# A decoder trunk on one core: the residual part of 18 weight tiles made by an adding DMA instead of a vector subtract

## The chip, the core and the metric

The kernel runs on one core of a Trainium2 chip. That core has five engines with a queue of instructions each: TensorE (PE, matrix products), VectorE (DVE), ScalarE (ACT), GpSimd (POOL) and SyncE (SP), and DMA engines that move data between the chip's memory and the core's SBUF. Each engine works through its queue in order; semaphores tie the queues together. PE writes to PSUM, eight banks of 128 x 512 fp32.

The metric is the device time of one execution in microseconds (us), the median over runs. The kernel before takes 1063.82 us (three runs, 1062.98 to 1064.26).

## The reference, cut to what matters

The input `x` is 512 tokens by 1024 channels, fp32. There are two residual layers, each a mixer and then an MLP:

```python
for l in range(2):
    h = rms_norm(x, mix_pre_g[l])
    y = even_mixer(h, ...) if l % 2 == 0 else odd_mixer(h, ...)
    x = x + rms_norm(y, mix_post_g[l])
    h = rms_norm(x, mlp_pre_g[l])
    x = x + rms_norm(sq_relu_mlp(h, mlp_w1[l], mlp_w2[l]), mlp_post_g[l])
```

The change lies in the first mixer:

```python
z = h @ w_in                                # 1024 -> 512 u, 512 q, 512 k, 512 v, 8 forget logits
y_a = s5_mixer(u, ..., w_glu)               # complex state-space scan, gelu, y * sigmoid(y @ w_glu)
y_b = fox_attention(q, k, v, fl, b_f)       # 8 heads of 64, causal, with a cumulative forget bias
return concatenate([y_a, y_b], -1) @ w_out  # 1024 -> 1024
```

The odd mixer has a pooling part and a gated part, the MLPs have 4096 inner channels and a squared ReLU. All results are fp32.

## The kernel before

**Products in three parts.** A product of fp32 matrices is made of three fast ones. Each operand is split into `hi`, its value rounded to the reduced format fp32r, and `lo`, what is left; `mm3` then adds up hi·hi, hi·lo and lo·hi in PSUM. `split` makes the two parts: ACT copies the source into `hi`, DVE subtracts `hi` from the source into `lo`. Activations and weights go through the same `split`.

**Weights.** A weight tile is 128 partitions by 1024 columns, 512 KB. Class `W` takes three buffers of SBUF for it: a raw one, which SP fills by a DMA, and two for the parts. The raw buffer is free again after the split. The list `plan` names all tiles in the order of their use: four tiles of `w_in_even` for v, then those for the steps in `ORDER` (q0, four of u, q1, q2, q3; a q step has one tile for the q and one for the k channels of two heads), two of `w_glu`, eight of `w_out_even` (rows 4 to 7 first), and then those of the MLPs and of the odd mixer. There are 47 buffers of 1024 columns for everything.

**The first mixer.** It starts with the normalization of x in four blocks of 128 tokens (`norm_T`): PE transposes a block, ACT and DVE split it into the parts that all later products read. Then come v (`token_block`), q and k of a pair of heads (`qk_block`), u (`step_u`), the constants of the state-space part on DVE and ACT (`step_z`, `step_c`, `step_o`, `step_e`, `step_t`), the forget bias (`step_f`), four scans over 128 channels each (`s5_run`) and the attention of four pairs of heads, interleaved, and at the end `w_glu` and the output product. POOL has little in it: it sets buffers to zero, and casts the bias rows into the keys (`KF`, two COPY rows per pair of heads).

**What sets the order.** The kernel doesn't issue as it is written. `Program.record` notes each operation (so that nearly every instruction has the line of this helper, L438, in the profile), and `Program.issue` puts them into the engines' queues by a list schedule: at each step of a simulated time it takes, for an engine that is free, the operation of best priority whose inputs are ready and whose buffers are to be had. The priority is made of the place in the program, the length of work behind it (`RANK`) and a bonus by step (`BOOST`, in thousands of ns; `u` for `step_u`, `q0` for the first `qk_block`, `W0` to `W3` for the weights of a phase). `LOOKS` limits how far ahead of its turn an operation may take a buffer, per phase: of SBUF, of PSUM, of SBUF by SP. The queue orders that come out are fixed in the program. The costs that it reckons with stand in `cost`, the times between engines in `LAT`.

## Time and profile before

| what | value |
|---|---|
| median of the runs | 1063.82 us |
| the profiled execution's own time | 1063.45 us |
| its span, first to last instruction | 1061.7 us, mean TensorE clock 0.993 |
| PE busy | 1039.3 us (98%) |
| DVE busy | 792.9 us (75%) |
| ACT busy | 568.5 us (54%) |
| POOL busy | 57.2 us (5%), 112 instructions |
| DMA | 104.53 MB, all transfers of weights issued by SP |

The shares are averages. The first mixer takes somewhat under a quarter of the span, the first MLP goes on to about 590 us, then come the odd mixer and the second MLP. Windows of the span give each engine's busy time in a stretch; a matmul counts as busy from its start to its modelled end, so a short wait between two can hide in PE's busy time. Names in the rows leave out buffer numbers: nearly every buffer is called `b`, a PSUM bank `bank`, the constants `ct`.

### The profile page before, as it was taken

The page shows a single profiled execution, that of the slowest core. Times are in us where ns is not written, and L with a number is a line of the kernel's source. Part 1 is how long each engine was busy: PE and PEld are TensorE (multiplying, and loading weights), DVE is VectorE, ACT ScalarE, POOL GpSimd, SP SyncE. Part 2 cuts the span into 40 slices and gives each one's busy share as a digit, 9 for nine tenths or more (in the row PEclk, how much of TensorE's full clock was granted, in tenths as well). Part 3 has the DMA queues.
Part 4 walks back from the last instruction along what each step waited for, and adds up shares of the span by engine and source line. Part 5 has one row for each costly group of instructions (what it writes and reads, how often), then busy time and mean ns, then how long its engine had stood idle before and what let it go on. Part 6 is the DMA issues. An engine that isn't in the chain of part 4 may idle for free.

```text
span 1061.7 us, 13872 instructions
## 1 busy us (share of the span) xinstructions
PE 1039.3 (98%) x5133; PEld 846.6 (80%) x5133; DVE 792.9 (75%) x1365; ACT 568.5 (54%) x1037; POOL 57.2 (5%) x112
## 2 busy tenths in 40 slices
PE   8999899999999999999999799999999999999996
PEld 5789677788988888888888688889888888888885
DVE  6968899759856586677778998566776697686786
ACT  5474978546744563553653644445645544553641
POOL 4001000003000000000001310011000000000001
PEclk9999999999999999999999899999999999999999
DMA  8221012623314322422514533306134225223212
GB/s 254 68 80 40 2 40 81 218 60 119 120 40 131 120 72 66 143 85 78 160 60 132 156 100 113 106 4 198 39 99 121 98 80 164 75 80 120 79 59 80
DMA packets 110385, 104.53 MB, mean 98 GB/s; under 512 B 9736, under 2 KB 92844, under 8 KB 110318
## 3 DMA queue, kind: packets, MB, share of 16 engines
q1 hardware_dynamic: 110318, 103.66, 31.8%
q8 instruction: 40, 0.66, 0.3%
q14 instruction: 27, 0.22, 0.1%
HBM read 101.55 MB, written 2.10 MB: 98 GB/s over the span
## 4 chain that ended last, share of the span: by engine, by line
PE 89%; ACT 5%; DVE 2%; SPq 1%; issue 1%; POOL 1%; DMA 0%; DVEq 0%; POOLq 0%; ACTq 0%
PE bank L438 89%; ACT b L438 5%; DVE b L438 2%; SPq L438 1%; POOL small L438 1%; DMA b<-in_x_dram 0%; ACT junk L438 0%; DVE small L438 0%; POOL b L438 0%; DVEq L1974 0%; POOLq L1974 0%; ACTq L438 0%; ACTq L1974 0%; DVEq L438 0%; POOLq L438 0%
## 5 line engine op out<-in xcount | busy, mean ns | idle before, releaser
L438 PE MATMUL bank<-b,b 128*128 128x512 f32 (+5 forms) x4684 | 1000.2, 376 | 8.9 <-DVE b L438 8.0
L438 PEld LDWEIGHTS bank<-b,b 128*128 128x128 f32 (+2 forms) x4684 | 810.3, 188 | 182.3 <-DVE b L438 7.2
L438 DVE TENSOR_TENSOR b<-b,b 128x1024 fp32r<-128x1024 f32 (+7 forms) x654 | 483.2, 775 | 128.8 <-ACT b L438 65.2
L438 ACT ACTIVATE b<-b 128x1024 fp32r<-128x1024 f32 (+6 forms) x582 | 376.1, 690 | 261.3 <-DVE b L438 121.9
L438 ACT ACTIVATE b<-bank 128x512 f32<-128x512 f32 (+7 forms) x269 | 131.3, 516 | 148.4 <-PE bank L438 138.2
L438 DVE TENSOR_TENSOR b<-bank,b 128x512 f32<-128x512 f32 (+2 forms) x210 | 120.7, 604 | 50.9 <-PE bank L438 30.9
L438 DVE TENSOR_TENSOR b<-b 128x256 f32<-128x256 f32 (+5 forms) x202 | 91.0, 466 | 36.0 <-PE bank L438 23.9
L438 POOL TENSOR_SCALAR small<-small 128x1 f32<-128x1 f32 x36 | 15.9, 443 | 852.9 <-ACT junk L438 836.7
L438 ACT ACTIVATE junk<-b 128x512 bf16<-128x512 f32 (+1 forms) x32 | 27.0, 843 | 43.5 <-DVE b L438 37.0
L438 PE MATMUL bank<-ct,b 128*128 128x128 f32 (+3 forms) x387 | 43.0, 260 | 5.0 <-DVE b L438 4.5
L438 DVE SCALAR_TENSOR_TENSOR b<-b,small,b 128x1024 f32<-128x1024 f32 (+1 forms) x32 | 36.4, 1150 | 14.8 <-POOL small L438 14.8
L438 PEld LDWEIGHTS bank<-ct,b 128*128 128x128 f32 (+3 forms) x387 | 33.9, 140 | 15.9 <-DVE b L438 6.1
L438 DVE SCALAR_TENSOR_TENSOR b<-b,b 128x512 f32<-128x512 f32 (+2 forms) x28 | 19.0, 686 | 13.9 <-ACT b L438 13.5
L438 POOL TENSOR_TENSOR small<-small,mhalf 128x1 f32<-128x1 f32 x36 | 26.7, 741 | 2.9
L438 ACT ACTIVATE b<-bank,small 128x128 f32<-128x128 f32 (+4 forms) x36 | 19.2, 545 | 7.4 <-DVE small L438 4.5
L438 ACT ACTIVATE junk<-bank 128x512 bf16<-128x512 f32 x16 | 9.5, 594 | 23.3 <-PE bank L438 23.0
L438 DVE TENSOR_REDUCE small<-bank 128x1 f32<-128x128 f32 (+3 forms) x32 | 14.0, 484 | 2.2 <-PE bank L438 2.0
L438 DVE SCALAR_TENSOR_TENSOR b<-b,bank 128x512 f32<-128x512 f32 x16 | 10.9, 681 | 4.8 <-ACT b L438 4.7
L438 POOL MEMSET b<- 128x4 f32 (+4 forms) x27 | 9.2, 375 | 78.7 <-ACT b L438 26.5
L438 DVE TENSOR_SCALAR b<-b,small 128x128 f32<-128x128 f32 (+3 forms) x28 | 9.9, 376 | 1.3 <-POOL small L438 1.1
L438 DVE TENSOR_TENSOR_SCAN b<-b,b 128x512 f32<-128x512 f32 x8 | 9.8, 1221 | 0.2
L438 POOL CAST b<-b 32x512 fp32r<-32x512 f32 (+1 forms) x8 | 5.3, 663 | 65.3 <-ACT b L438 64.9
(41 smaller groups left out, 97.8 us busy)
## 6 DMA issues: line engine op xcount, KB each, us to landing
b<-in_mlp_w_dram SPq DMA_DIRECT2D x128, 512.0 KB, 4.4
b<-in_w_in_even_dram SPq DMA_DIRECT2D x16, 512.0 KB, 6.7
b<-in_w_in_odd_dram SPq DMA_DIRECT2D x12, 512.0 KB, 4.2
b<-in_w_out_even_dram SPq DMA_DIRECT2D x8, 512.0 KB, 3.5
b<-in_w_out_odd_dram SPq DMA_DIRECT2D x8, 512.0 KB, 3.5
b<-in_x_dram SPq DMA_DIRECT2D x7, 512.0 KB, 5.3
out_dram<-b SPq DMA_DIRECT2D x8, 256.0 KB, 2.0
b<-in_s_w_glu_dram SPq DMA_DIRECT2D x2, 512.0 KB, 3.7
```

What stands on the lines that cost most here:

```text
L438: o.ins = o.fn(*args, **kw)
```

## The change

Class `Added` replaces `W` for 18 tiles: the four of u, the eight of q0 to q3, the two of `w_glu` and four of `w_out_even`. The raw tile is loaded by SP and ACT copies it to `hi` as before. Then ACT copies it a second time with a scale of -1 into `lo`, which gives minus `hi`, and a DMA that POOL issues reads the same tile from the chip's memory once more and adds it onto `lo`, which gives the raw value minus `hi`. The subtract on DVE is gone. Each of these tiles has one ACT copy and one DMA more and one DVE instruction less.

The list schedule gets a cost for that DMA, which is issued on POOL. A term of the priority with weight zero (`DUE`) is taken out with the code that worked it out. `LOOKS` and `BOOST` have new values, which sets a new order in all phases.

```diff
-LOOKS = {0: (202, 21, 10), 1: (186, 29, 7), 2: (48, 11, 15), 3: (36, 8, 6)}
+LOOKS = {0: (97, 21, 21), 1: (63, 42, 7), 2: (18, 17, 11), 3: (31, 10, 2)}
...
-    "q1": -20, "q3": -5, "q0": 120, "u": -5, "S5D": -20, "s0": 40, "t": 5, "z": -25, "q2": -25, "a0": 85, "a1": 10,
...
+    "q1": -60, "q3": -15, "q0": 110, "u": 40, "S5D": 15, "s0": 20, "t": 5, "z": -65, "q2": -65, "a0": 55, "a1": 10,
...
         if eng == "POOL":
+            if name == "dma_start":
+                return 1550
...
-                o.prio = (1 - DUE) * (o.prio * (1 - RANK) * UNIT - RANK * o.rank) + DUE * o.due - 1e3 * o.boost
+                o.prio = o.prio * (1 - RANK) * UNIT - RANK * o.rank - 1e3 * o.boost
...
+                    elif o.name == "dma_start":
+                        clock[e] = now + o.ns
+                        dma = max(dma, clock[e]) + 5000
+                        o.end = dma + 3000
...
     class W:
+        by_dma = False
+
...
             SP.dma_start(raw.f().rearrange("p (a b) -> p a b", a=shape[0]), src)
-            split(raw.f(), self.b[0].r(), self.b[1].r())
+            hi, lo = (b.r() for b in self.b)
+            if self.by_dma:
+                act(hi, raw.f(), AF.Copy)
+                act(lo, raw.f(), AF.Copy, scale=-1.0)
+                G.dma_start(lo.rearrange("p (a b) -> p a b", a=shape[0]), src, accum_op=ALU.add)
+            else:
+                split(raw.f(), hi, lo)
...
+    class Added(W):
+
+        by_dma = True
...
-            plan += [rows(we, 256 * k, 2, 0, 512) for k in range(4)]
+            plan += [rows(we, 256 * k, 2, 0, 512) + (Added,) for k in range(4)]
...
-            plan += [rows(we, 0, 8, 512 + 128 * hp, 128), rows(we, 0, 8, 1024 + 128 * hp, 128)]
-    plan += [rows(w_glu[0], 256 * k, 2, 0, 512) for k in range(2)]
-    plan += [rows(w_out_even[0], 128 * k, 1, 0, 1024) for k in (4, 5, 6, 7, 0, 1, 2, 3)]
+            plan += [rows(we, 0, 8, 512 + 128 * hp, 128) + (Added,), rows(we, 0, 8, 1024 + 128 * hp, 128) + (Added,)]
+    plan += [rows(w_glu[0], 256 * k, 2, 0, 512) + (Added,) for k in range(2)]
+    plan += [rows(w_out_even[0], 128 * k, 1, 0, 1024) + ((Added,) if k in (4, 5, 6, 7) else ()) for k in (4, 5, 6, 7, 0, 1, 2, 3)]
```

Three places of the new order follow. In a row stand the helper's line, the operation, the buffer that is written, behind the arrow those that are read, and the shape; the number behind the underscore tells values in one buffer apart.

**ACT at the start, before.** Rows of 128x2x128 are splits of x (blocks i=2 and i=3), those of 128x1024 the `hi` copies of q0's two tiles and of u's tiles, those of 128x512 results of v.

```order
L438 ACTIVATE b33_359<-b35_225 128x1024
L438 ACTIVATE b29_192<-bank5_346 128x2x128
L438 ACTIVATE b31_198<-bank5_346 128x2x128
L438 ACTIVATE b25_183<-bank3_368 128x2x128
L438 ACTIVATE b27_186<-bank3_368 128x2x128
L438 ACTIVATE b36_384<-b38_253 128x1024
L438 ACTIVATE b48_308<-bank0_234 128x512
L438 ACTIVATE b39_400<-b41_262 128x1024
L438 ACTIVATE b29_192<-bank6_402 128x2x128
L438 ACTIVATE b31_198<-bank6_402 128x2x128
```

**The same place now**, two copies to a tile (those of q0, and of the first three tiles of u):

```order
L434 ACTIVATE b34_361<-b35_118 128x1024
L434 ACTIVATE b33_379<-b35_118 128x1024
L434 ACTIVATE b37_400<-b38_120 128x1024
L434 ACTIVATE b36_419<-b38_120 128x1024
...
L434 ACTIVATE b46_495<-b47_227 128x1024
L434 ACTIVATE b45_499<-b47_227 128x1024
L434 ACTIVATE b29_184<-bank2_350 128x2x128
L434 ACTIVATE b31_189<-bank2_350 128x2x128
L434 ACTIVATE b25_168<-bank1_393 128x2x128
L434 ACTIVATE b27_174<-bank1_393 128x2x128
L434 ACTIVATE b29_184<-bank3_427 128x2x128
```

All ten copies, which read five tiles (b35, b38, b41, b44, b47), now stand ahead of the last six splits of x; before, the second and the third tile's copies stood among these splits, and those of the fourth and fifth behind them.

**POOL between the first and the second pair of heads, now.** The COPY rows are `KF` (32 and 64 partitions, into the keys), the DMA rows the adds onto the `lo` parts of q1's two tiles, q2's two and q3's first.

```order
L434 DMA b81_771<-in_w_in_even_dram 128x8x128
L434 MEMSET b148_1007 128x4
L434 MEMSET b140_1037 128x1024
L434 MEMSET b141_1052 128x1024
L434 COPY b136_1165<-b55_764 32x512
L434 DMA b99_1149<-in_w_in_even_dram 128x8x128
L434 COPY b136_1165<-b55_764 64x512
L434 DMA b102_1203<-in_w_in_even_dram 128x8x128
L434 DMA b105_1223<-in_w_in_even_dram 128x8x128
L434 MEMSET b175_1243 128x4
L434 DMA b108_1237<-in_w_in_even_dram 128x8x128
L434 MEMSET b142_1275 128x4
```

Before, this queue held no DMA; the COPY and MEMSET rows stood next to each other.

**DVE at the boundary of the layers, before.** The rows of 128x2x128 are splits of the first token block for the odd mixer, the row of 128x512 is the last `collect` of the MLP, which adds a PSUM bank to a result and so frees the bank.

```order
L438 TENSOR_TENSOR b706_5359<-b707_5303,b705_5345 128x1024
L438 TENSOR_TENSOR b694_5301<-bank5_5348,b693_5281 128x2x128
L438 TENSOR_TENSOR b696_5308<-bank5_5348,b695_5287 128x2x128
L438 TENSOR_TENSOR b384_3299<-bank4_5002,b384_3299 128x512
L438 TENSOR_TENSOR b698_5311<-bank2_5353,b697_5290 128x2x128
L438 TENSOR_TENSOR b700_5321<-bank2_5353,b699_5294 128x2x128
L438 SCALAR_TENSOR_TENSOR b715_5381<-b275_2268,small_123,b692_5164 128x1024
```

**The same place now:**

```order
L434 TENSOR_TENSOR b706_5370<-b707_5321,b705_5355 128x1024
L434 TENSOR_TENSOR b694_5319<-bank3_5358,b693_5299 128x2x128
L434 TENSOR_TENSOR b696_5326<-bank3_5358,b695_5305 128x2x128
L434 TENSOR_TENSOR b698_5329<-bank6_5363,b697_5308 128x2x128
L434 TENSOR_TENSOR b700_5335<-bank6_5363,b699_5312 128x2x128
L434 TENSOR_TENSOR b384_3317<-bank2_5020,b384_3317 128x512
L434 SCALAR_TENSOR_TENSOR b715_5390<-b275_2179,small_124,b692_5182 128x1024
```

The `collect` (into b384) has moved behind the last two splits.

More of the change, by code (lines that the diff above doesn't have):

```diff
@@ L41 @@
 RANK = 0.55
-DUE = 0.0
 ORDER = "f z c q0 a0 u e o q1 t s0 a1 s1 q2 a2 s2 q3 a3 s3".split()
@@ L301, in issue @@
             o.rank = o.ns + max((s_.rank + self.LAT[o.eng][s_.eng] for s_ in o.succs), default=0.0)
-        at = 0.0
-        for o in ops:
-            o.due = at
-            if o.eng == "PE":
-                at += o.ns
-        for o in reversed(ops):
-            own = o.due if o.eng == "PE" or not o.succs else math.inf
-            o.due = min([own] + [s_.due - self.LAT[o.eng][s_.eng] - o.ns for s_ in o.succs])
         for o in ops:
             if o.eng != "SP":
-                o.prio = (1 - DUE) * (o.prio * (1 - RANK) * UNIT - RANK * o.rank) + DUE * o.due - 1e3 * o.boost
+                o.prio = o.prio * (1 - RANK) * UNIT - RANK * o.rank - 1e3 * o.boost
                 if o.banks and o.eng != "PE":
```

8 rows, old and new, of the table BOOST are left out of this document.

## The prediction

> **What bounds the kernel now.** I read the page first, for the busy shares and the chain of waits.
>
> ```profile
> PE 1039.3 (98%) x5133; PEld 846.6 (80%) x5133; DVE 792.9 (75%) x1365; ACT 568.5 (54%) x1037; POOL 57.2 (5%) x112
> PE 89%; ACT 5%; DVE 2%; SPq 1%; issue 1%; POOL 1%; DMA 0%; DVEq 0%; POOLq 0%; ACTq 0%
> ```
>
> TensorE (PE) is busy for 1039.3 of 1061.7 us, and the change leaves its work alone. Time can be won or lost only where PE stands still, or runs below its rate, for want of another engine. Windows of the span show where that is.
>
> ```profile
> core 0: us, PE busy (x) PEld busy (x) DVE busy (x) ACT busy (x) POOL busy (x), PEclk, DMA share, GB/s
> 0.00:50.00 50.00, 46.89 (x202) 32.34 (x203) 40.48 (x158) 26.75 (x55) 10.89 (x25) 1.00 0.59 171
> 100.00:150.00 50.00, 46.20 (x296) 34.54 (x296) 43.96 (x92) 41.50 (x102) 3.44 (x12) 0.97 0.04 12
> 250.00:300.00 50.00, 50.00 (x319) 45.17 (x318) 43.60 (x71) 34.12 (x66) 3.55 (x6) 1.00 0.28 91
> 550.00:600.00 50.00, 44.39 (x196) 35.89 (x195) 44.02 (x65) 26.45 (x46) 6.72 (x15) 0.93 0.47 144
> 130.00:202.00 72.00, 70.42 (x457) 53.01 (x457) 67.61 (x139) 55.81 (x118) 0.42 (x4) 0.98 0.22 72
> ```
>
> PE has gaps at the start, from 100 to 150 us, and at the boundary between the layers (550 to 600); the row at 250 stands for the MLP stretches, where PE is busy for all 50.00. The last row decides: from 130 to 202 us the S5 scans and the attention blocks run together, and DVE is busy for 67.61 of 72.00 us, 94%. That PE shows 70.42 hides its loss, since a matmul that starts a fraction late is counted as a longer one. DVE sets this stretch, with ACT at 55.81 behind it. The chain of waits, here a few of its pieces, shows that just ahead of it ACT is the one.
>
> ```profile
> 115.18 0.31 ACT b L438
> 120.27 0.31 ACT b L438
> 143.41 17.75 PE bank L438 x126
> ```
>
> From 107 to 143 us small ACT copies of 0.31 to 0.8 us end last one after another (those of `step_t`, `step_o` and the first scan); after that the chain lies mostly on PE.
>
> **What moves.** Each of the 18 tiles loses one DVE subtract and gains one ACT copy, both 128x1024. First such pairs over the run, then those inside 130 to 202 us.
>
> ```profile
> L438 DVE TENSOR_TENSOR b<-b,b 128x1024 fp32r<-128x1024 f32 x198 | 239.9, 1222 | 80.2 <-PE bank L438 41.1 <-ACT b L438 30.5 <-issue 7.4
> L438 ACT ACTIVATE b<-b 128x1024 fp32r<-128x1024 f32 x198 | 204.8, 1055 | 100.0 <-DVE b L438 59.8 <-PE bank L438 22.9 <-DMA b<-in_mlp_w_dram 12.3
> L438 DVE TENSOR_TENSOR b<-b,b 128x1024 fp32r<-128x1024 f32 x7 | 8.4, 1218 | 0.0
> ```
>
> That is 18 x 1.222 = 22.0 us off DVE and 18 x 1.055 = 19.0 us onto ACT. Where neither ends last, it is worth nothing. Five places count.
>
> **1. The scans, 130 to 202 us.** The seven subtracts of the third row are the last tile of q3, both of w_glu and the first four of w_out_even, all Added now, so DVE goes to 67.61 - 8.4 = 59.2 us. Seven more copies bring ACT to 55.81 + 7 x 1.055 = 63.2 us: ACT is then the busier one. If it fills the stretch as far as DVE does now, 67.61 / 72.00 = 0.939, the stretch takes 63.2 / 0.939 = 67.3 us, 4.7 less. If the copies fit into ACT's holes (they wait for a load alone, not for the scan), all of DVE's 8.4 us comes off. Between 4.7 and 8.4 I take **-6.5**.
>
> **2. The start.** In the order all ten copies of the first five Added tiles stand on ACT ahead of the last splits of x, which PE needs to go on; before, the tiles' copies stand between those splits.
>
> ```profile
> 20.00:30.00 10.00, 9.52 (x49) 7.65 (x48) 8.84 (x44) 7.49 (x19) 1.72 (x4) 1.00 1.06 322
> 30.00:40.00 10.00, 10.00 (x47) 8.21 (x46) 10.00 (x53) 3.93 (x7) 0.00 (x0) 1.00 0.06 6
> 30.16 0.60 PE L438 MATMUL bank<-ct,b 128*128 128x128 f32 x4
> 30.51 5.75 PE L438 MATMUL bank<-b,b 128*128 128x512 f32 x24
> 26.09 1.06 ACT L438 ACTIVATE b<-b 128x1024 fp32r<-128x1024 f32 x1
> 30.79 0.66 ACT L438 ACTIVATE b<-bank 128x256 fp32r<-128x256 f32 x2 [0.16 <-PE bank L438]
> 16.33 5.17 DMA b<-in_x_dram
> ```
>
> The loads run at 322 GB/s until 30 us and at 6 GB/s after it, so the fifth tile is there at about 30.5. Its two copies (2 x 1.055), half of the ACT row of two splits (0.33) and as much again on DVE give 33.3 us for PE's next matmul. By the order 62 matmuls of 512 columns of v lie ahead of this stop; before, 63 lie ahead of the transposes at 30.16, so PE comes to it then: **+3.1**. The rows of x that are now loaded ahead (the chain waits on x for 5.17 us at 16.33) don't help, as PE only comes to this stop earlier. Lower bound: the fifth tile 1.5 us sooner, as SP wastes less, +1.6. Upper: two adds of 512 KB share the queues with the loads, 2 x 0.52 MB / 322 GB/s = 3.2 us more, +6.3.
>
> **3. PE's stop at 59.4** goes, since the subtract in front of the copy that PE waits for leaves DVE:
>
> ```profile
> 57.69 1.23 DVE L438 TENSOR_TENSOR b<-b,b 128x1024 fp32r<-128x1024 f32 x1 [0.28 <-ACT b L438]
> 58.83 0.42 DVE L438 COPY b<-b 128x512 f32<-128x512 f32 x1
> 59.40 1.16 PE L438 MATMUL bank<-b,b 128*128 128x512 f32 x3 [1.18 <-DVE b L438]
> ```
>
> The copy of 58.83 can then come 1.23 us sooner: **-1.2** (0, if step 2 makes PE that late anyway).
>
> **4. Ahead of `step_t`.** Eight copies of four q tiles (8 x 1.055 = 8.4 us) now stand on ACT just before and between the first pieces of the ACT chain.
>
> ```profile
> 107.23 4.42 ACT L438 ACTIVATE b<-bank 64x128 f32<-64x128 f32 x16 [5.79 <-PE bank L438]
> ```
>
> ACT is idle for 5.79 us there, which hides most of them; the rest has 8.4 - 5.79 = 2.6 us to push the chain, less what begins earlier: **+0.5** (0 to 2.6).
>
> **5. The boundary.** DVE's last `collect` of the MLP now stands behind all four splits of a row block and not behind two.
>
> ```profile
> 592.51 2.50 PE L438 MATMUL bank<-b,b 128*128 128x512 f32 x5 [3.36 <-DVE b L438]
> 591.11 2.01 DVE L438 TENSOR_TENSOR b<-bank,b 128x256 fp32r<-128x256 f32 x5
> ```
>
> Two splits of 2.01 / 5 = 0.40 us are what its bank waits longer: **+0.8** (0 to 0.8, as PE gets the splits sooner in exchange).
>
> **The adds themselves** have no row: no transfer in the trace is issued by POOL. The nearest are the plain loads of the same tiles:
>
> ```profile
> b<-in_w_in_even_dram SPq DMA_DIRECT2D x16, 512.0 KB, 6.7
> b<-in_w_out_even_dram SPq DMA_DIRECT2D x8, 512.0 KB, 3.5
> L438 POOL CAST b<-b 32x512 fp32r<-32x512 f32 (+1 forms) x8 | 5.3, 663 | 65.3 <-ACT b L438 64.9
> ```
>
> An add reads a tile from HBM as a load does, and the lo part besides. Lower bound 3.5 us (idle queues), upper 2 x 6.7 = 13.4 (busy ones, twice the traffic). I take 6.7 while loads run, and cost it at nothing: its cover is the PE work between the copy and the first use of lo. That cover is thin at one spot only: q0's first tile, copied at 26.09, has its lo at 26.1 + 1.1 + 6.7 = 33.9 us, and PE asks for it 11 matmuls of 0.24 (5.75 / 24) after the stop of step 2, at 35.9. On POOL an add waits for its copy, and behind it stand `KF` casts (0.663 us each) and memsets. POOL is busy for 57.2 of 1061.7 us, so I cost the issue at nothing too.
>
> The Trainium skill, "DMA: Bandwidth & Descriptors", section on the anatomy of a DMA of the gpsimd path, fits such a transfer by 2.0 us plus the bytes at 436 GB/s; for 512 KB that is 3.2 us, an estimate, near the 3.5 of the idle queue, and no run here shows it for an adding one. With it the sum stays and the slower rival falls.
>
> Sum: -6.5 + 3.1 - 1.2 + 0.5 + 0.8 = -3.3. The profiled execution took 1063.45 us (span 1061.7 and 1.75 around it), so 1060.15; the median of the runs lies 0.37 above it, which gives **1060.5**.
>
> **Rivals.** A change below 0.2%, 2.1 us, can't be told from none here.
>
> *The gain is given back* (1063.5). ACT fills the scans' stretch only as DVE does now (-4.7), and the start's +3.1 passes to the end whole, step 3 swallowed in it: -4.7 + 3.1 + 0.5 + 0.8 = -0.3. For it: ACT is at 63.2 of 72.0 by the sum above, and the pieces of 0.31 us are ACT's. Against: copies of weights have no input but the load.
>
> *Slower: the adds come one after another and too late for u* (1065.7). Six adds, q0's two and u's four, go out from 27.2 us on. If they run in turn and take t each, the sixth ends at 27.2 + 6 t. PE asks for that lo 113 matmuls of 512 columns after q0's first (27.1 us at 0.24) and some 4 us of smaller ones, at about 67. From t = 6.6 us on PE waits; at 7.5 us for 5.2, so 1060.5 + 5.2. For it: the median of 6.7 of a plain load there, and twice its traffic. Against: loads share 16 engines and overlap, so adds may. The same rule would make the four adds of q tiles near 105 us late for their `qk` blocks.
>
> The Trainium skill, "SBUF — State Buffer", section "Who interferes with whom", says that a transfer issued by GpSimd can be starved of descriptor writing while a DVE instruction holds the port pair they share. DVE's 10.00 of 10.00 us at 30 to 40 would be its place; no trace here shows it.
>
> *A larger gain* (1055.5): all of DVE's 8.4 comes off, and the start is absorbed behind PE's later stops: -8.4 - 1.2 + 0.5 + 0.8 = -8.3. For it: PE's losses from 100 to 150 us.
>
> *The change is not what decides*: new looks and boosts reorder all phases. Against: PE is busy for 50.00 of 50.00 in the MLPs, so reordering there can win nothing and can lose only what buffers hold up. Either sign, within 4 us.
>
> **Chances.** The forecast 0.34, gain given back 0.27, slower by late adds 0.22, larger gain 0.13, reordering 0.04. Faster by over 0.2%: most of the forecast (0.30), the larger gain (0.13) and 0.03 of the rest, 0.46. Within: 0.27, of the second and the fringes. Slower: 0.22 and 0.05 of the fringes, 0.27. The forecast's own range is 1057.5 to 1062.5, by the bounds of steps 1 and 2. To leave out no more than 2 in 10 it reaches to 1055 on the side of the larger gain and to 1067.5 on the other, past the late adds at 7.5 us.
>
> **What would show it.** Step 1: from the first scan to the last the windows hold about 65 us of time, with ACT above 60 us busy and DVE near 59. Step 2: PE stands still for about 3 us near 30, with ACT named. Step 3: no stop at `step_f`'s copy. Step 4: the chain's ACT pieces start not over 1 us later relative to PE. Step 5: the boundary's stop at 4.2 in place of 3.36. Late adds would show as PE waits on a transfer from w_in_even. Wrong is the forecast if DVE's share in the scans stays at 94%, or if PE waits at the start for more than 6 us.

## The result and the profile after

The changed kernel took 1071.28 us in the median (1070.22 to 1073.43, 4 runs), the kernel before 1063.66 (1062.98 to 1064.26) beside it: a ratio of 1.0073 with a 95% interval of 1.0060 to 1.0085. It is slower by 7.6 us. The forecast was 1060.5 and the range ended at 1067.5, so both missed. The profiled execution, the fastest of the four, took 1070.22 us, with a span of 1068.4 against 1061.7 before, so 6.7 us are to be found in the trace.

The page's busy times and the shares of the chain of waits:

```profile
PE 1037.1 (97%) x5133; PEld 846.1 (79%) x5133; DVE 776.9 (73%) x1347; ACT 584.8 (55%) x1055; POOL 81.9 (8%) x130
PE 85%; DVE 6%; ACT 4%; POOL 2%; issue 2%; DMA 1%; SPq 0%; DVEq 0%; POOLq 0%; ACTq 0%
```

The work moved as announced: 18 instructions fewer on DVE and 16 us less (22.0 reckoned), 18 more on ACT and 16 us more (19.0 reckoned). The chain, however, gives 6% to DVE where it gave 2%. The windows, in the form shown of before (PE, weight loads, DVE, ACT, POOL; granted clock; DMA share; GB/s):

```profile
0.00:50.00 50.00, 40.22 (x166) 27.76 (x167) 36.10 (x158) 30.82 (x63) 17.73 (x28) 0.93 0.93 223
138.00:209.00 71.00, 67.61 (x456) 51.49 (x457) 64.76 (x135) 63.19 (x128) 8.85 (x15) 1.00 0.54 137
550.00:600.00 50.00, 43.61 (x197) 35.34 (x197) 41.38 (x60) 25.47 (x45) 6.57 (x12) 0.96 0.44 138
```

The first row carries most of the loss: 40.22 us of PE in the first 50, where there were 46.89, 166 matmuls in place of 202, and a clock of 0.93. The second row is the scans and the attention, aligned by PE's work: 456 matmuls in 71 us, where 130 to 202 us held 457 in 72. The boundary's row is little changed.

To place the rest I lined PE up with itself: each matmul counts for the usual pitch of its shape (the median time from its start to the next one's, in the kernel before), and at equal amounts of such work done I compare when PE got there. A number is how much later (us) than in the kernel before; e1 to e16 are the experiments below.

```
work done (before's time)  after   e1    e2    e3    e5    e6   e16    e9   e10    e7    e8
  20  ( 24.9)               2.5   4.3   0.6   6.0   1.6   1.7   1.1   2.4   4.2  -0.5   0.3
  30  ( 35.0)               9.1   4.3   6.5   6.0   7.8   2.0   1.9   9.3  11.5  -0.6   0.3
  50  ( 55.3)               9.1   5.1   7.3   6.7   7.7   5.3   2.8   9.2  11.5  -0.6   0.2
  70  ( 76.2)               7.9   4.7   8.0   6.5   6.6   4.1   1.6   8.0  10.4  -0.6   0.2
  90  ( 96.1)               9.0   5.0   7.9   6.0   7.7   5.3   2.7   9.1  11.5  -0.6   0.2
 120  (125.0)               8.8   5.9  10.9   6.3   7.4   5.0   2.5   8.9  11.2  -0.6   0.2
 150  (161.4)               8.0  16.6  16.0  11.5   8.3   5.8   3.3  10.5  13.0  -0.4   1.2
 190  (201.8)               7.0  16.8  21.9  11.5   7.3   4.8   2.3   9.5  11.9  -0.4   8.9
 540  (554.4)               6.2  17.7  22.6  12.2   6.5   4.1   2.1   8.8  11.2  -0.4  16.7
 600  (620.5)               7.1  17.7  22.8  12.7   7.4   5.0   3.2   9.7  12.1  -0.1  16.7
1020 (1042.2)               6.4  16.5  22.5  10.5   6.8   4.6   4.1   8.9  11.6  -0.1  16.8
```

So the changed kernel loses 9.1 us in its first 35, wins 1.2 between 35 and 76 us (where the stop at 59.4 was), gives 0.9 back by 125, wins 1.8 in the scans (work 120 to 190), loses 0.9 at the boundary, and wins 0.8 and 0.7 in the two MLP stretches. Where the two kernels give PE its matmuls in another order, the table is no finer than about 1 us: from 76 to 96 us the lag grows from 7.9 to 9.0, and PE has no stop there in either trace. Only the loss at the start is well above that.

The loss at the start, PE's instructions of the changed kernel from 10 to 46 us:

```profile
16.03 1.32 PE L434 MATMUL bank<-ct,b 128*128 128x128 f32 x8 [1.50 <-DVE b L434]
21.61 1.43 PE L434 MATMUL bank<-b,b 128*128 128x512 f32 x5 [0.53 <-DVE b L434]
30.96 2.99 PE L434 MATMUL bank<-b,b 128*128 128x512 f32 x12
38.11 8.14 PE L434 MATMUL bank<-b,b 128*128 128x512 f32 x25 [4.17 <-ACT b L434]
```

PE has worked off what is ready at 33.95 and stands still for 4.17 us, until 38.11, for ACT. ACT in the same stretch:

```profile
26.45 11.35 ACT L434 ACTIVATE b<-b 64x256 f32<-64x256 f32 x14
37.70 2.69 ACT L434 ACTIVATE b<-bank 128x256 fp32r<-128x256 f32 x8
```

The first row is 14 instructions without a gap: four of `step_c` and then the ten 128x1024 copies of five Added tiles. ACT waits for no load there; it is simply not through. Only behind them come the six splits of x that PE needs. And behind the stop TensorE runs at half its rate (windows at 30, 38 and 41 us):

```profile
30.00:40.00 10.00, 5.83 (x25) 4.42 (x24) 9.25 (x51) 10.00 (x17) 6.48 (x5) 0.80 1.13 183
38.00:41.00 3.00, 2.89 (x7) 2.31 (x8) 2.64 (x8) 2.54 (x9) 0.32 (x1) 0.50 1.22 233
41.00:44.00 3.00, 3.00 (x11) 2.39 (x10) 2.90 (x9) 0.00 (x0) 0.00 (x0) 0.71 1.13 206
```

ACT is busy for 10.00 of 10.00 us. A granted clock of 0.50 over 2.9 us and 0.71 over 3.0 costs 2.9 x 0.5 + 3.0 x 0.29 = 2.3 us. That makes 4.2 for the stop, 2.3 for the clock and 2.5 that PE was late already at 25 us: 9.0 of the 9.1. The Trainium skill, "TensorE: Matmul & The Clock Gate", section "What's actually happening", says that the clock falls to half after an idle window of about 3.4 us; the 0.50 behind a stop of 4.17 us agrees with it. The length of a stop doesn't settle it in these traces, though: behind a stop of 2.67 us the kernel before has 0.54 (129 to 132 us), behind one of 1.67 us e6 has 0.62 (56 to 59 us), and behind one of 3.45 us the changed kernel has 1.00 (139 to 142 us).

### The profile page after: what moved, and what is told of

Read it like the earlier page. It is cut to its first block, busy times and chain, and to the rows that moved or that the text cites. A ratio compares the mean times of both kernels' runs of the same rounds, so it can differ in the third digit from the quotient of the medians.

```text
span 1068.4 us, 13902 instructions
## 1 busy us (share of the span) xinstructions
PE 1037.1 (97%) x5133; PEld 846.1 (79%) x5133; DVE 776.9 (73%) x1347; ACT 584.8 (55%) x1055; POOL 81.9 (8%) x130
## 4 chain that ended last, share of the span: by engine, by line
PE 85%; DVE 6%; ACT 4%; POOL 2%; issue 2%; DMA 1%; SPq 0%; DVEq 0%; POOLq 0%; ACTq 0%
PE bank L434 85%; DVE b L434 6%; ACT b L434 2%; POOL small L434 2%; ACT junk L434 1%; DMA b<-in_mlp_w_dram 0%; DMA b<-in_w_in_even_dram 0%; POOL b L434 0%; SPq L434 0%; DVE small L434 0%; DVEq L1982 0%; POOLq L1982 0%; ACTq L434 0%; DVE mag L434 0%; DVE mst L434 0%
## 5 line engine op out<-in xcount | busy, mean ns | idle before, releaser
L434 PE MATMUL bank<-b,b 128*128 128x512 f32 (+6 forms) x4684 | 998.8, 376 | 15.7 <-DVE b L434 9.5
L434 DVE TENSOR_TENSOR b<-b,b 128x1024 fp32r<-128x1024 f32 (+10 forms) x636 | 463.4, 763 | 129.8 <-ACT b L434 83.3
L434 ACT ACTIVATE b<-b 128x1024 fp32r<-128x1024 f32 (+5 forms) x600 | 393.2, 701 | 231.3 <-DVE b L434 115.5
L434 ACT ACTIVATE b<-bank 128x512 f32<-128x512 f32 (+6 forms) x269 | 131.0, 517 | 179.8 <-PE bank L434 178.3
L434 DVE TENSOR_TENSOR b<-b 128x512 f32<-128x512 f32 (+5 forms) x202 | 90.4, 462 | 38.7 <-ACT b L434 21.9
L434 POOL TENSOR_SCALAR small<-small 128x1 f32<-128x1 f32 x36 | 20.3, 565 | 829.3 <-ACT junk L434 808.4
L434 DVE SCALAR_TENSOR_TENSOR b<-b,small,b 128x1024 f32<-128x1024 f32 (+1 forms) x32 | 36.4, 1149 | 13.8 <-POOL small L434 13.8
L434 POOL TENSOR_TENSOR small<-small,mhalf 128x1 f32<-128x1 f32 x36 | 23.1, 641 | 3.0
L434 POOL DMA_DIRECT2D b<-in_w_in_even_dram x12 | 17.4, 1450 | 38.8 <-ACT b L434 32.4
L434 POOL MEMSET b<- 128x4 f32 (+4 forms) x27 | 10.1, 395 | 59.4 <-PE bank L434 25.8
```

The source lines that it names most:

```text
L434: o.ins = o.fn(*args, **kw)
```

## The experiments

Each is timed against the kernel before on the same chip. Where letters stand in the expectations, S is the theory that the start costs the time, T that the order of the tables does as such, D that late or crowding adds do, and P the rival by which DVE doesn't bound the scans.

### Is DVE what bounds the scans? (e7, e10)

e7 is the kernel before, in its own order, without the seven DVE subtracts of the scans (PE reads the hi part in place of lo).

```diff
+NOLO = (16, 17, 18, 19, 20, 21, 22)
...
-            o.ins = o.fn(*args, **kw)
+            if o.tag and o.tag[0] in NOLO and o.eng == "ACT":
+                o.tag[3].t.ap = o.tag[5].t.get()
+            if not (o.tag and o.tag[0] in NOLO and o.eng == "DVE"):
+                o.ins = o.fn(*args, **kw)
```

> The kernel before in its own order, with seven DVE subtracts of 1.22 us left out between 130 and 202 us (the last tile of q3, w_glu, four of w_out_even); PE reads hi where it read lo, so the lo part of these seven tiles is left out of the result. DVE is relieved with no copy and no add in exchange: the most that step 1 can be worth. The prediction's theory (DVE sets this stretch): -6 to -8.4, 1055.5 to 1058. Theory P (PE's own work fills it: a sum of the matmuls' usual pitches there gives 70 us, the stretch with its first stop 76.8): -1 to -3, 1060.8 to 1063.

It took 1063.59 us (10 runs, 1063.13 to 1064.45): ratio 1.000 [0.999, 1.001]. The window that the first step of the prediction went by, in e7:

```profile
130.00:202.00 72.00, 70.41 (x456) 53.10 (x455) 61.22 (x132) 55.41 (x117) 0.42 (x4) 0.98 0.23 74
```

DVE fell from 67.61 to 61.22 us, and PE did 456 matmuls where it did 457. The relief that step 1 priced at 4.7 to 8.4 us is worth nothing by itself. The times in brackets in the table show why. For 30 units of work (120 to 150) PE takes 36.4 us, from 125.0 to 161.4; for the next 40 it takes 40.4. So nearly all that PE loses in this stretch lies ahead of 161 us. The first row is PE of the kernel before, the second its window behind the stop:

```profile
129.82 4.56 PE L438 MATMUL bank<-b,b 128*128 128x128 f32 x25 [2.67 <-DVE b L438]
129.00:132.00 3.00, 2.18 (x8) 2.02 (x9) 2.99 (x5) 2.96 (x4) 0.10 (x1) 0.54 0.00 0
```

The stop of 2.67 us, 1.3 us for the clock behind it (0.54, then 0.89 from 132 to 135 us) and three stops of 0.19, 0.60 and 0.28 us up to 143.4 make 5.1 of the 6.8 us by which 76.8 exceeds 70. e7 has the same stop, of 2.65 us. Of the seven subtracts one stands at 130.19 and the others at 170.45 or later, where DVE is busy but PE doesn't wait for it.

e10 asks the same of ACT, in the changed kernel: the same seven tiles have neither second copy nor add.

```diff
+            if o.tag and o.tag[0] in NOLO:
+                first, other = (o.tag[1], o.tag[2]) if o.args[0].t is o.tag[1] else (o.tag[2], o.tag[1])
+                if o.eng == "POOL" or first.ap is not None:
+                    continue
+                other.ap = first.get()
...
```

> The changed kernel in its own order, but the seven Added tiles of the scans' stretch (the last of q3, w_glu, four of w_out_even) have neither the second copy nor the add; PE reads hi where it read lo, so these tiles' low parts are left out of the result. ACT is relieved of 7 x 1.055 = 7.4 us there. If ACT has taken DVE's place in the scans (the rival of the prediction): 3 to 5 us less, 1066 to 1068.5. Theory P (PE's own work fills the stretch, and neither engine's copies matter): within 1 us of the changed kernel, 1070 to 1072.

It took 1073.08 us (1071.32 to 1075.41), ratio 1.0085 [1.0068, 1.0102]. From work 120 to 190 PE loses 0.7 us where the changed kernel wins 1.8, so freeing ACT brings nothing there either. By 35 us e10 is 2.4 behind the changed kernel; the first 1.7 of it are a hold on DVE that the last section shows.

The 1.8 us themselves are not the tiles' doing. All seven profiles with this order in the scans (the changed kernel, e4, e5, e6, e9, e10, e16) have the same stop of 3.44 to 3.46 us for DVE there, longer than the 2.67 of before. Behind it the same 24 matmuls take 3.13 us in the changed kernel and 4.45 to 5.57 in the other six. PE and the window behind the stop, first of the changed kernel, then of e9:

```profile
140.05 3.13 PE L434 MATMUL bank<-b,b 128*128 128x128 f32 x24 [3.45 <-DVE b L434]
139.00:142.00 3.00, 1.95 (x15) 1.80 (x16) 2.87 (x5) 2.93 (x7) 0.00 (x0) 1.00 0.00 0
140.17 5.55 PE L436 MATMUL bank<-b,b 128*128 128x128 f32 x24 [3.45 <-DVE b L436]
139.00:142.00 3.00, 1.83 (x7) 1.77 (x8) 2.94 (x5) 2.93 (x6) 0.05 (x1) 0.50 0.00 0
```

The clock stayed at 1.00 in this one execution and fell to 0.50 in e9's. So between work 120 and 150 the changed kernel wins 0.8 us, and the five of the others that are in the table lose 0.8 to 1.8; from 150 to 190 all six win 1.0 or 1.1. The full clock there was luck of the profiled execution; what decides it was not tested.

### The start (e4, e5, e6, e16)

e4 puts the six copies of u's first three tiles, and their adds, behind the last six splits on ACT; DVE is left as it is.

```diff
...
+        last = max(i for i, o in enumerate(order) if o.tag == "X" and o.eng == "ACT")
+        late = [o for o in order[:last] if o.tag in ('W2', 'W3', 'W4')]
+        held = set(id(o) for o in late)
+        order = [o for o in order[:last + 1] if id(o) not in held] + late + order[last + 1:]
...
```

> The changed kernel in its own order, but for one edit: the six copies of the first three tiles of u, with their adds, stand behind the last six splits of x and not ahead of them. All 18 tiles stay Added. Theory S: the splits come 6.3 us sooner, PE's stop of 4.17 goes and with it the stretch at half clock: 1064 to 1067. Theories T and D: 1070 to 1072, since neither the rest of the order nor the traffic changes.

It took 1070.94 us (1070.23 to 1073.22), ratio 1.0072 [1.0057, 1.0087]: no better than the change. ACT, then DVE, then PE of e4:

```profile
33.77 1.73 ACT L441 ACTIVATE b<-bank 128x256 fp32r<-128x256 f32 x6
```
```profile
36.75 2.66 DVE L441 TENSOR_TENSOR b<-b,b 128x256 f32<-128x256 f32 x7
39.34 2.07 DVE L441 TENSOR_TENSOR b<-bank,b 128x256 fp32r<-128x256 f32 x6
```
```profile
39.80 8.52 PE L441 MATMUL bank<-b,b 128*128 128x512 f32 x24 [3.44 <-DVE b L441]
```

ACT's splits are done 4 us sooner, but DVE's halves of the same splits stand in its line behind a long run of small instructions of the S5 setup, and come at 39.34. PE's stop is 3.44 us, and its releaser is now DVE. A split has two halves, and the new order had set both back.

e5 moves only four memsets of `step_o` to the head of POOL. e6 moves, on top of that, the six splits ahead on ACT and on DVE.

```diff
...
+        early = [o for o in order if o.tag == "O"]
+        rest = [o for o in order if o.tag != "O"]
+        at = min(i for i, o in enumerate(rest) if o.eng == "POOL" and o.name == "tensor_scalar")
+        order = rest[:at] + early + rest[at:]
# e6 besides:
+        at = max(i for i, o in enumerate(order) if o.tag == "X" and o.eng == "PE")
+        late = [o for o in order[at + 1:] if o.tag == "X"]
+        order = order[:at + 1] + late + [o for o in order[at + 1:] if o.tag != "X"]
...
```

> The changed kernel in its own order, but for four POOL memsets of 128x1024 (for step_o) that go back to the head of POOL's queue, where they stand in the kernel before. Theory M: in the changed kernel they run from 14.06 to 17.7 us, and a small DVE TENSOR_SCALAR of 0.17 us that meets them takes 1.03 us (2.69 to 3.6 in three of the experiments so far), so PE stops for 1.5 to 4 us at 14 to 18 us, with a stretch at half clock behind the longer ones. Without them: no stop at 16 us, 1 to 3 us come back, 1067.5 to 1070. If the memsets have nothing to do with it: 1071.

> The kernel with the early memsets, and with the last six splits of x moved ahead in both queues: on ACT ahead of the copies for u, on DVE ahead of the small operations of step_z and step_e that stood in front of them (moving ACT's part alone won nothing: DVE's part then came at 39 us, behind those). Theory S: now PE's stop near 34 us goes, and the half clock after it: 5 to 6.5 us less than with the early memsets alone, 1061.5 to 1064. Theory D (traffic and lateness of the adds): no gain, since the lo parts of q0 come no sooner, 1067 or more.

e5 took 1070.41 us (1069.09 to 1070.71), ratio 1.0060 [1.0045, 1.0075]: 0.9 to 1.3 us better in PE's progress at 25 and 35 us, 0.9 in the median, where the two intervals overlap. e6 took 1067.20 (1065.92 to 1068.36), ratio 1.0031 [1.0019, 1.0043]. With the splits ahead, PE's lag at 35 us is 2.0 in place of e5's 7.8: **5.8 us of the loss are the splits' place in the two queues**. PE of e5 and of e6:

```profile
37.24 19.92 PE L441 MATMUL bank<-b,b 128*128 128x512 f32 x78 [4.18 <-ACT b L441]
30.13 21.29 PE L444 MATMUL bank<-b,b 128*128 128x512 f32 x90
```

Of the 5.8 us 3.3 come back at 53 us, so that the time lands where theory D had put it (1067 or more), though not for D's reason: the stop that S named is gone. PE, DVE and ACT of e6:

```profile
53.09 0.42 PE L444 MATMUL bank<-ct,b 16*128 16x16 f32 x4 [1.67 <-DVE b L444]
```
```profile
37.85 8.24 DVE L444 TENSOR_TENSOR b<-b,b 128x256 f32<-128x256 f32 x22
```
```profile
46.05 4.85 ACT L444 ACTIVATE b<-bank 64x512 fp32r<-64x512 f32 x8 [6.33 <-DVE b L444]
```

The 22 instructions on DVE are now later, ACT waits 6.33 us for them, and PE for what follows: a new wait, with a slower clock behind it. e16 tests whether DVE is too full there: e6 without the three subtracts of v's tiles at 17 to 22 us (PE reads the hi part).

```diff
+NOLO = (2, 3, 4)
...
+            if isinstance(o.tag, tuple) and o.tag[0] in NOLO:
+                if o.eng == "DVE":
+                    continue
+                o.tag[2].ap = o.tag[1].get()
```

> The kernel with early memsets and splits first (1067.2), less three DVE subtracts of 1.22 us at 17 to 22 us (v's tiles two to four; PE reads hi where it read lo, so their low parts are left out of the result). If DVE's full queue from 10 to 46 us causes the stop near 53 us: it shrinks or goes, 2 to 3.5 us less, 1063.5 to 1065.5. If the adds of u cause it: unchanged, 1066.5 to 1068.

1067.90 us (1067.39 to 1069.72), ratio 1.0037 [1.0025, 1.0049]: the median isn't better. By its time the first expectation failed. In the trace, though, the stop shrinks to 0.87 us and the lag at 55 us to 2.8, as it said; but another wait turns up, and from work 540 on e16 loses 2.0 us where e6 loses 0.5. PE of e16:

```profile
35.56 15.76 PE L449 MATMUL bank<-b,b 128*128 128x512 f32 x67 [0.59 <-DMA b<-in_w_in_even_dram]
52.19 0.41 PE L449 MATMUL bank<-ct,b 16*128 16x16 f32 x4 [0.87 <-DVE b L449]
```

The first fits the thin cover of q0's first tile that the prediction named: e16's first add goes out at 27.85 us, and its adds take 7.7 in the median, which gives 35.55. It is seen only where PE is no longer held up ahead of it. Why the later phases of e16 lose was not settled.

### The adds (e9, e3)

e9 is the changed kernel with adds of 512 bytes in place of 512 KB.

```diff
+            if o.eng == "POOL" and o.name == "dma_start":
+                args = [args[0][0:1, 0:1, 0:128], args[1][0:1, 0:1, 0:128]]
```

> The changed kernel in its own order, but each of the 18 adds moves 512 bytes instead of 512 KB, so lo is left at minus hi nearly everywhere (the low parts of these weights are left out of the result). The order, the copies and the issues on POOL stay. Theory D (the adds' traffic, 9.4 MB, or lo parts that land late): 2 to 6 us less than the changed kernel, 1065 to 1069. Theory S (the order of ACT's and DVE's queues at the start): within 0.7 of the changed kernel, 1070.5 to 1072.

1073.18 us (1069.72 to 1074.20), ratio 1.0078 [1.0060, 1.0096], with the same stop of 4.16 us for ACT: the stop is not of the adds' making, and without their bytes and their lateness the time is no lower. By work 120 PE's lag is 8.9 us, and 8.8 with the full adds; the difference behind that is the clock at 140 us, shown above. The rows of the transfers on the changed kernel's page (count, KB, median us to landing), and its DMA instructions on POOL:

```profile
b<-in_w_in_even_dram POOLq DMA_DIRECT2D x12, 512.0 KB, 7.6
b<-in_w_out_even_dram POOLq DMA_DIRECT2D x4, 512.0 KB, 7.7
b<-in_w_out_even_dram SPq DMA_DIRECT2D x8, 512.0 KB, 7.1
L434 POOL DMA_DIRECT2D b<-in_w_in_even_dram x12 | 17.4, 1450 | 38.8 <-ACT b L434 32.4
```

An add takes 7.6 us to land, 6.7 had been taken and 3.5 to 13.4 bounded; the estimate of 3.2 us that the prediction gave beside it, by the fit of the Trainium skill, "DMA: Bandwidth & Descriptors", section on the anatomy of a DMA of the gpsimd path, is less than half of what was measured. An add occupies POOL for 1.45 us. A plain load of w_out_even beside them takes 7.1 where it took 3.5 before, and 4.3 in e9.

e3 leaves q0 and u plain, with 12 Added tiles.

```diff
-            plan += [rows(we, 256 * k, 2, 0, 512) + (Added,) for k in range(4)]
+            plan += [rows(we, 256 * k, 2, 0, 512) for k in range(4)]
...
+            kind = (Added,) if hp else ()
...
```

> The changed kernel with q0's two and u's four tiles made by copy and subtract again; the twelve later tiles stay Added. Theory S: the start is that of the tables alone, 6 to 7 us come back (the stop of 4.17 and the half clock behind it), the scans keep their 2 us of gain: 1063 to 1066. Theory T: 1070. Theory D: a third of the adds is gone, those in the busiest stretch: 1066 to 1069.

1073.15 us (1071.93 to 1074.49), ratio 1.0086 [1.0069, 1.0102], against what the start's theory expected. The stop at 34 to 38 us is gone. But 6.0 us are lost by 25 us, to the memsets, and a further 5 between work 120 and 150, where the list schedule came out otherwise too: PE stops there for 3.93 and 2.03 us, in place of 3.45 and 1.12. An edit of the tiles moves the schedule with it, so such an experiment doesn't isolate a tile.

### Order without tiles, tiles without order (e1, e2, e8)

e1 keeps the new tables with all tiles plain; e2 keeps the 18 Added tiles with the tables of before.

```diff
# e1
-        by_dma = True
+        by_dma = False
# e2
-LOOKS = {0: (97, 21, 21), 1: (63, 42, 7), 2: (18, 17, 11), 3: (31, 10, 2)}
+LOOKS = {0: (202, 21, 10), 1: (186, 29, 7), 2: (48, 11, 15), 3: (36, 8, 6)}
# and BOOST as before
...
```

> The new LOOKS and BOOST alone: no tile is Added, all 18 are made by copy and subtract, so the arithmetic is that of before in a new order. Theory S (the start: ten copies of 1.06 us stand on ACT ahead of the last splits of x, and PE stops for them): five copies instead of ten, interleaved with the splits as in the kernel before, so the stop of 4.17 us at 34 us is gone; 1063 to 1066. Theory T (the new order itself costs the time, whatever makes lo): 1069 or more. Theory D (the adds' traffic and lateness cost it): no adds, so 1062 to 1065.

> All 18 tiles Added, LOOKS and BOOST of the kernel before. Theory S: in this order eight copies in a row stand ahead of five of the splits as well, so PE stops there again: 1067 to 1073. Theory T: the old order is good, so 1058 to 1062. Theory D: 1068 to 1073, and the loss lies in waits for lo, not at the splits.

e1: 1079.25 us, ratio 1.0143 [1.0128, 1.0159]. e2: 1084.40, ratio 1.0197 [1.0182, 1.0212]. Either half alone is worse than both by 8 to 13 us. e1 is late by 4.3 at the start and loses 10.7 between work 120 and 150, in stops for DVE and ACT such as these two of its PE:

```profile
140.16 4.62 PE L434 MATMUL bank<-b,b 128*128 128x128 f32 x23 [4.17 <-DVE b L434]
168.59 0.79 PE L434 MATMUL bank<-b,b 128*128 128x512 f32 x1 [3.54 <-ACT b L434]
```

That the new order leans on the relief of DVE, and falls behind without it, fits the first of these stops, but was not taken apart. PE of e2:

```profile
36.89 19.84 PE L434 MATMUL bank<-b,b 128*128 128x512 f32 x74 [3.50 <-ACT b L434]
```

The start's stop is there under the old tables too, and is missing in e1 and e3: it comes with Added tiles at the start, not with the new tables.

e8 asks what the adds are worth where no list schedule rearranges anything: before's order, the seven tiles of the scans Added at the place of their copy or, if later, where lo's buffer comes free.

```diff
...
+            if o.tag and o.tag[0] in ADDED and o.eng == "DVE":
+                pass
+            else:
+                o.ins = o.fn(*args, **kw)
+            for n, src, a, lo, raw, _ in spots.get(at[id(o)], ()):
+                self.engines["ACT"].activation(lo.real(), raw.real(), AF.Copy, scale=-1.0)
+                self.engines["POOL"].dma_start(lo.real().rearrange("p (a b) -> p a b", a=a), src, accum_op=ALU.add)
```

> The kernel before in its own order, with the same seven tiles made by the second copy and the adding DMA, both put right behind the tile's first copy; nothing else moves. The prediction's step 1: -4.7 to -8.4, 1055.5 to 1059. Theory P: between -2 and +1, 1062 to 1065. If the adds harm by themselves (late lo, traffic): 1066 or more.

1080.03 us (1078.44 to 1081.26), ratio 1.0152 [1.0137, 1.0167]. PE's two stops for a transfer, and the last of the adds on POOL:

```profile
186.55 5.08 PE L453 MATMUL bank<-b,b 128*128 128x512 f32 x27 [2.54 <-DMA b<-in_w_out_even_dram]
220.42 2.50 PE L453 MATMUL bank<-b,b 128*128 128x512 f32 x5 [6.12 <-DMA b<-in_w_out_even_dram]
```
```profile
209.40 0.85 POOL L456 DMA_DIRECT2D b<-in_w_out_even_dram  x1 [20.27 <-ACT b L455]
```

Here the adds are late: lo's buffer comes free too near to its use, and a subtract of 1.2 us fits there where an add, of 5.8 to 6.9 us in the medians, doesn't. The last one goes out at 209.40, and PE goes on at 220.42. Not all of the 16.7 us is that: from 130 to 225 us PE waits 8.7 us for these adds, and 4.9 for ACT, where it waited 0.7 before.

### The single stop at 59.4 us (e11, e12)

e11 is the kernel before with the subtract of u's fourth tile exchanged with the copy of `step_f` behind it on DVE. e12 makes that one tile Added, its copies in ACT's idle time ahead.

```diff
# e11
+        cut = next(i for i, o in enumerate(order) if o.tag and o.tag[0] == TILE and o.eng == "DVE")
+        nxt = next(i for i in range(cut + 1, len(order)) if order[i].eng == "DVE")
+        order.insert(nxt, order.pop(cut))
# e12
...
+        order = [o for o in order if o is not hi and o is not cut]
+        order.insert(spot + 1, hi)
...
+                self.engines["ACT"].activation(lo.real(), raw.real(), AF.Copy, scale=-1.0)
+                self.engines["POOL"].dma_start(lo.real().rearrange("p (a b) -> p a b", a=a), src, accum_op=ALU.add)
```

> The kernel before, with one pair of DVE instructions swapped: the subtract of u's fourth tile (1.23 us at 57.69) behind the copy of step_f for which PE stops 1.18 us at 59.40. If that stop is worth what the prediction's step 3 says, and PE does not need the tile's lo at once: 0.5 to 1.2 us less, 1062.5 to 1063.2. If the stop is swallowed later, or PE then waits for lo instead: 1063.4 to 1064.2.

> The kernel before with that one tile Added: its first copy moves ahead in ACT's queue, into ACT's idle 5.45 us before 53.8, the second copy and the add stand right behind it, the subtract leaves DVE. One add where ACT idles and the queue is empty. If step 3 holds and the add lands before PE asks (issue near 51.5, 6 to 7.6 us to land, asked for near 59): 1 to 1.4 us less, 1062.4 to 1062.8, faster than both kernels. If the add is late by a us or two: 1063 to 1065, and PE is seen to wait for it.

e11: 1063.39 us (11 runs), ratio 0.9992 [0.9983, 1.0001]. e12: 1063.47, ratio 0.9990 [0.9981, 0.9998]. In both the stop is gone; PE of e12 runs through it:

```profile
53.62 4.21 PE L453 MATMUL bank<-ct,b 128*64 128x128 f32 x110
57.76 1.19 PE L453 MATMUL bank<-b,b 128*128 128x512 f32 x3
59.04 6.74 PE L453 MATMUL bank<-b,b 128*128 128x384 f32 x29
```

Both gain 1.2 us of progress there. The Added tile gains no more than two instructions exchanged.

### The tables of the later phases (e13, e14, e15)

The kernel before, with the new tables for phases 1 and 3 (e13), with u's fourth tile Added besides (e14), and with those of phases 1, 2 and 3 (e15).

```diff
-LOOKS = {0: (202, 21, 10), 1: (186, 29, 7), 2: (48, 11, 15), 3: (36, 8, 6)}
# e13, e14
+LOOKS = {0: (202, 21, 10), 1: (63, 42, 7), 2: (48, 11, 15), 3: (31, 10, 2)}
# e15
+LOOKS = {0: (202, 21, 10), 1: (63, 42, 7), 2: (18, 17, 11), 3: (31, 10, 2)}
# and BOOST of these phases in all three
...
```

> The kernel before with the changed kernel's LOOKS and BOOST for the two MLP phases alone; the first mixer keeps its order, no tile is Added. If the gains of 0.8 and 0.7 us that PE's progress shows in the MLPs of the changed kernel are the tables' own: 1062 to 1063. The prediction's price for the MLPs (nothing to win where PE is busy for 50.00 of 50.00): 1063.4 to 1064.3.

> The same tables with u's fourth tile Added as in the run with that tile alone (0.999 of before). If the two add up: 1061 to 1062.3, below both kernels by more than the noise. If not: 1063 to 1064.

> As the first of these, with the changed kernel's tables for the odd mixer as well, so the boundary between the layers has the changed order (the collect behind four splits). The prediction's step 5: 0.8 us more than without, so 1062.8 to 1064. If the boundary's +0.9 belongs to the late arrival from the first mixer and not to the order: as without, 1062 to 1063.

e13: 1064.59 us, ratio 1.0005 [0.9996, 1.0014]. e14: 1062.66 (11 runs, 1061.66 to 1063.90), ratio 0.9985 [0.9977, 0.9994]. e15: 1065.70, ratio 1.0010 [1.0001, 1.0019]. The new tables of the later phases gain nothing; that of phase 2 costs about 1.1 us (e15 less e13). e15 did not get the order at the boundary that its expectation counts on: in its trace the `collect` still stands between the two pairs of splits (shown under step 5 below). e14 is the fastest of all, ahead of both kernels, but by 0.15%, inside the 0.2% that the prediction counted as no change; with 11 runs its interval does exclude 1. Why it is faster, while e13's tables alone are not, the traces don't show.

## Why the prediction was wrong, by its steps

**Step 2, the start, is the term that decided: +9.1 where +3.1 was written, bounds 1.6 to 6.3.** The prediction saw the right place, the right releaser and the right rows, and reckoned the stop from the wrong end: from the last load's arrival and the two copies behind it. ACT was never waiting for a load. It had four instructions of `step_c` and ten copies to do in line, 11.35 us, and was through at 37.8, not at 33. The stop is 4.17 us, near the expected 3. The half clock behind it (2.3) and a lag of 2.5 at 25 us had not been in the sum at all. e6 shows 5.8 of the 9.1 to be the splits' place; e5 shows about 1 to be the memsets; the rest of the early lag, some 1.6 us, is the new order's and was not taken apart.

**Step 1, the scans, failed in its reason: -6.5 foreseen, -1.8 in the profiled execution, and less elsewhere: with the same order e5 gets -0.1 there, e9 +0.6.** "DVE sets this stretch" was read from a busy share of 94%. e7 takes the seven subtracts away and gains 0.0 us; e10 takes ACT's seven copies away and gains nothing. What PE loses there is one stop of 2.67 us at 127 us, the clock behind it, and three short stops by 143 us; behind 161 us it runs at its pitch, and there most of the relief fell. The prediction had the piece in hand: its chain of waits went through small ACT copies up to 143 us and then lay mostly on PE. Its remark that a late matmul is counted as a long one hid this reading. Its test, "wrong if DVE's share stays at 94%", was met in part (64.76 of 71.00, 91%; near 59 had been expected, and ACT came to 63.19 as reckoned). Even the -1.8 was luck: the changed order has a longer stop at that place, 3.45 us, and only the clock, which did not fall behind it in the profiled execution, made up for it. What ends that first stop sooner was not tried, and 1.7 of the 6.8 us by which the scans exceed PE's pitch stay open.

**Step 3 was right** in mechanism and size: the stop is gone. The lag of the changed kernel, which falls by 1.2 by 76 us and is back at 9.0 by 96, can't show the size, as its PE takes the work in another order; e11 and e12, which keep the order, show the 1.2 at the spot. Over the whole run about 0.1% is left of it.

**Step 4 was harmless as foreseen.** Between 90 and 120 units of work PE's lag goes from 9.0 to 8.8 us, so the eight copies cost nothing that can be told from the +0.5.

**Step 5 was right** in mechanism and size, +0.9 for +0.8. The boundary's two stops in the changed kernel's PE, and the `collect` (the DVE row of 128x512) in the kernel before, in the changed kernel and in e15:

```profile
594.19 1.09 PE L434 MATMUL bank<-ct,b 128*128 128x128 f32 x8 [2.37 <-DVE b L434]
599.30 1.65 PE L434 MATMUL bank<-b,b 128*128 128x512 f32 x3 [4.02 <-DVE b L434]
```
```profile
591.78 0.68 DVE L438 TENSOR_TENSOR b<-bank,b 128x512 f32<-128x512 f32 x1
598.56 0.68 DVE L434 TENSOR_TENSOR b<-bank,b 128x512 f32<-128x512 f32 x1
592.28 0.68 DVE L432 TENSOR_TENSOR b<-bank,b 128x512 f32<-128x512 f32 x1
```

4.02 stands where 3.36 stood, 4.2 had been named. In all three PE goes on 0.05 or 0.06 us after the `collect` ends (592.51, 599.30 and 593.02 us). It starts 1.32 us after the first split in the changed kernel and 0.67 in the kernel before: 0.65 us later, and the stop grew by 0.66. In e15 it starts 0.66 after it, as before, so e15's 1.1 us have another cause, which stays open.

**The adds** cost the changed kernel nothing that e9 could win back, as the prediction had put it. The slower rival had the right sign and the wrong mechanism: adds too late are real in e8, where a stop of 6.12 us names one, but not in the changed kernel. The rival nearest to the truth was the last, "the change is not what decides", with a chance of 0.04 and "within 4 us": e1 and e2 show the order, and tiles that don't fit it, moving the time by 15 and 20 us.

The forecast's own range, 1057.5 to 1062.5, doesn't come out of the bounds that it names: with both bounds of steps 1 and 2 it is 1057.1 to 1065.5. The result lies outside either.

## What to carry to other kernels

A busy share, even 94%, doesn't say that an engine sets the time. Look first where in the stretch PE stands still; an experiment that leaves the engine's work out then settles it, and costs one run. To say when an in-order engine delivers, add up everything in its line ahead of the instruction that is waited for, on each engine that makes a part of it, and then the clock behind the stop; the last input's arrival is only a lower bound. An add took 7.6 us to land, so it needs that much cover, and an idle engine for its copies; where both held (e12), it gained 1.2 us at the spot, and exchanging two instructions did as much. One profiled execution can be lucky: a stop that the clock happens to pass over looks like a gain.

## What had not been expected of the hardware

A small DVE instruction can be held for several memsets of POOL. Around 14 us POOL clears four buffers; DVE has 128x16 instructions beside it, which take 0.17 us elsewhere. DVE of the changed kernel, of e1, of e3 and of e5 (where the memsets come earlier), and POOL of the changed kernel and of the kernel before:

```profile
13.92 1.12 DVE L434 TENSOR_SCALAR b<-b 128x16 f32<-128x16 f32 x2
15.07 0.88 DVE L434 TENSOR_SCALAR b<-b 128x16 int32<-128x16 int32 x1
```
```profile
13.92 2.90 DVE L434 TENSOR_SCALAR b<-b 128x16 f32<-128x16 f32 x2
```
```profile
13.94 3.79 DVE L434 TENSOR_SCALAR b<-b 128x16 f32<-128x16 f32 x2
```
```profile
13.92 0.25 DVE L441 TENSOR_SCALAR b<-b 128x16 f32<-128x16 f32 x2
```
```profile
14.06 3.68 POOL L434 MEMSET b<- 128x1024 f32 x4
```
```profile
L438 POOL MEMSET b<- 128x1024 f32 x5 | 4.6, 958 | 0.0
```

A memset takes 3.68 / 4 = 0.92 us. The two TENSOR_SCALARs take 0.25 us undisturbed (e5) and 0.87, 2.65 and 3.54 us more in the others, which is one, three and four memsets. PE's stop behind them is 1.50, 3.28 and 4.10 us (0.56 in e5). In the kernel before, five memsets of this size, 0.96 us each, and some smaller ones were over by 6.7 us, ahead of these instructions. The early memsets of e5 hold another one: a CAST of 128x128 at 2.82 us takes 3.80, where it takes 0.23 in the changed kernel; by 13 us DVE is level again. One order of instructions can show different holds: the changed kernel and e9 had 1.12 in their profiled runs, e4 and e10, with the same order there, 2.90. This fits the wide spread of the kernels of that order (1069.7 to 1075.4 us, e5 1069.1 to 1070.7), to which the clock in the scans may add its part. The Trainium skill, "SBUF — State Buffer", section "Who interferes with whom", says that DVE's two-port modes, which a tensor_scalar can enter, and GpSimd lock each other out for a whole instruction. The lengths agree with whole memsets; that the wait can span three or four of them, the runs add.
